# Eight weight loads, four parts of each kind and four gate tiles for the filling work that follows attention, in a one-core hybrid RWKV-7 / latent-attention block

## The chip, the core and the metric

The kernel runs on one core of one Trainium2 chip. The metric is device time in microseconds (us): the median of several runs of the same program. One further execution was taken with the hardware profiler; its rows are what the prediction argues from. The engines are called as the profile calls them: PE (matrix multiply; its loading of the stationary operand is the row PEld), DVE (vector), ACT (scalar), POOL, and SP, which issues nearly all transfers here. A wait at the head of SP's queue holds everything behind it.

## What is computed

One layer of a hybrid block on 256 latent and 256 context tokens, D = 2048. Each normed and modulated stream goes through one wide projection; one branch is a bidirectional RWKV-7 scan, the other a multi-head latent attention; both are projected to D and merged by sigmoid gates, and an output projection and a gated residual follow. What matters here is the merge at the end:

```python
def merge_branches(o_rwkv, o_mla, gate_logits, w_br_r, w_br_m, w_out):
    g_r, g_m = jnp.split(jax.nn.sigmoid(gate_logits), 2, axis=-1)
    return (g_r * (o_rwkv @ w_br_r) + g_m * (o_mla @ w_br_m)) @ w_out
...
        (rkv_x, zr_x, wd_x, ad_x, qd_x, kvd_x, kr_x, zm_x, mg_x) = project_stream(x, norm_w[i], sh_x, sc_x, w_in[i])
...
        x_new = x + g_x * merge_branches(o_rw_x, o_ml_x, mg_x, w_branch_rwkv[i], w_branch_mla[i], w_out[i])
```

`gate_logits` is `mg_x`, the last 2 x 2048 columns of the wide projection. The RWKV output `o_rw_x` is known before attention begins, the attention output only when attention is done.

## The kernel before

**Split operands.** Every large product is made of three fp32r matmuls. A weight piece `w` (128 x 512 fp32, 256 KB) is loaded by SP (`piece`, L217), then `parts_of` makes two parts of it: ACT casts the high part `wh`, DVE subtracts to give the low part `wl` (both recorded at the helper's line L122). `mm3` then issues activation-high x weight-high, activation-high x weight-low and activation-low x weight-high (L103). A piece of four 128-column blocks thus gives 12 matmuls of 128 x 256 in the work described here, and PE needs both parts of a piece before it can finish the first three of them.

**Buffers.** The list `place` says where `w`, `wh` and `wl` live and how many of each there are. It begins as `[wp, NW, NSP, NSL]`: pool `wp`, 4 loads, 3 high parts, 2 low parts. The numbers `NWL, NSX, NSX` = 8, 4, 4 are used in the pool `mg`, which is opened when attention's pool `ml` has been given back.

**Stages.** After the RWKV part (with its background projections) comes attention, in pool `ml`, until 1090 us. Beside it runs a generator `background()`, `bg`, that is advanced by `next(bg)` between steps of attention and issues *filling work*:

- `merge_gate_g(i)`: one 128-column block of the gate logits. Four pieces of `w_proj`, 48 matmuls into an `acc` tile, then ACT's tanh into a tile `th`, stored to DRAM as `thd[i]` (L454). It yields after every sixth matmul, and so takes eight steps and an end.
- `branch_g(j)`: block j of the RWKV output's projection. It loads the gate `thd[j]` back into a `th` tile (L1376), loads two pieces of `w_br[0, j]`, does 24 matmuls into `acc`, multiplies on DVE (`th = (th + 1) * acc`) and stores `th` to `thd[j]` again (L1385). There are 16 of these.

When attention is done, `for _ in bg: pass` issues all of the filling work that is left: four `merge_gate_g` blocks not yet begun on PE, and all 16 `branch_g` blocks. All of it draws on `place` as it stands, with four loads, three high and two low parts; `th` has two buffers in `wp`. So the third `th` load must wait until the first tile has been multiplied and its store has landed.

**The merge loop** `for j in range(KT)` then does block j of the attention output's projection: two pieces of `w_br[1, j]`, two gate loads `gth0`, `gth1` (L1425), 24 matmuls into `chp`, four DVE steps and a cast that write `mh`, `mlo`. At `j == 2` it sets `place[:] = mg, NWL, NSX, NSX`. After it the output projection runs over 64 pieces of `w_out`, 6 matmuls of 128 x 512 each.

**What sets the order.** The program is written in one order, and a scheduler places each engine's instructions; loads may be placed well ahead of their use where their buffer is free. `gx` and `xr` (256 KB each, L1441 and L1452) are loads for the very end.

Of the kernel before, what the change touches and what calls it, by code (L numbers as in the profile page):

```python
# [9 lines left out]
F32 = mybir.dt.float32  # L10
# [6 lines left out]
P = 128  # L17
D = 2048
KT = D // P
T = 256  # L20
# [32 lines left out]
NW, NSP, NSL, NWL, NSX, NWU, UN, NWM = 4, 3, 2, 8, 4, 4, 2, 11  # L53
# [73 lines left out]
def hybrid_block(  # L127
# [27 lines left out]
    wp = ctx.enter_context(tc.tile_pool(name="wp", bufs=2))  # L155
# [42 lines left out]
    def split(src, hi, lo):  # L198

        S.copy(hi, src)  # L200
        V.tensor_tensor(lo, src, hi.bitcast(F32), ALU.subtract)
# [10 lines left out]
    place = [wp, NW, NSP, NSL]  # L212
# [15 lines left out]
    def weights(src, n, pool=None, ns=None):  # L228

        ws = [piece(src[:, n // 2 * i:n // 2 * i + n // 2], [P, n // 2], pool) for i in range(2)]  # L230
        for w in ws:
            yield parts_of(w, pool, ns)

    def mm3(ps, ah, al, bh, bl, start, stop):

        E.matmul(ps, lhsT=ah, rhs=bh, start=start, stop=False)
        E.matmul(ps, lhsT=ah, rhs=bl, start=False, stop=False)
        E.matmul(ps, lhsT=al, rhs=bh, start=False, stop=stop)
# [334 lines left out]
    with tc.tile_pool(name="rw", bufs=1) as rw:  # L573
# [507 lines left out]
        def background():  # L1081

            while main or extra:
                ready = next((m for m in main if m[0]()), None)
                if ready:
                    main.remove(ready)
                    task = ready[1]
                elif extra:
                    task = extra.pop(0)
                else:  # L1090
                    yield False
                    continue
                for r in task:
                    yield True
                yield True

        bg = background()
# [36 lines left out]
    with tc.tile_pool(name="ml", bufs=2) as ml:  # L1134
# [227 lines left out]
        def bring():  # L1362
# [7 lines left out]
            nonlocal brought  # L1370
            brought = True

        def branch_g(j):

            th = wp.tile([P, T], F32, name="th", tag="th", bufs=2)
            nc.sync.dma_start(th, thd[j])  # L1376
            ps = pp.tile([P, 512], F32, name="acc", tag="acc", bufs=2)
            for i, (wh, wl) in enumerate(weights(w_br[0, j], 1024)):
                for k in range(4):
                    cs = slice(128 * k, 128 * k + 128)  # L1380
                    mm3(ps[:, 0:T], wh[:, cs], wl[:, cs], *(t[:, 4 * i + k] for t in ob[0]), i + k == 0, i * 4 + k == 7)
                    if k % 2:
                        yield
            V.scalar_tensor_tensor(th, th, 1.0, ps[:, 0:T], ALU.add, ALU.mult)
            nc.sync.dma_start(thd[j], th)  # L1385

        brought = False
        for j in range(KT):
            main.append(((lambda j=j: brought and len(extra) == 0), branch_g(j)))
# [14 lines left out]
    mg = ctx.enter_context(tc.tile_pool(name="mg", bufs=2))  # L1404
    ob.append(halfs(mg, [P, 8, T], "ob", 1))
    for q in range(2):
        qs = slice(4 * q, 4 * q + 4)
        split(omla[:, qs], *(t[:, qs] for t in ob[1]))
    for _ in bg:
        pass  # L1410
    while gate_left:
# [6 lines left out]
    mh = mg.tile([P, KT, T], F32R, name="mh", bufs=1)  # L1418
    ml_ = mg.tile([P, KT, T], F32R, name="mlo", bufs=1)
    for j in range(KT):  # L1420
        if j == 2:
            place[:] = mg, NWL, NSX, NSX
        th = [mg.tile([P, T], F32, name=f"gth{b}") for b in range(2)]
        for b in range(2):
            nc.sync.dma_start(th[b], thd[16 * b + j])  # L1425
        ps = pp.tile([P, 512], F32, name="chp", tag="ch", bufs=2)
        for i, (wh, wl) in enumerate(weights(w_br[1, j], 1024)):
            for k in range(4):
                cs = slice(128 * k, 128 * k + 128)
                mm3(ps[:, 0:T], wh[:, cs], wl[:, cs], *(t[:, 4 * i + k] for t in ob[1]), i + k == 0, i * 4 + k == 7)  # L1430
        t = mg.tile([P, T], F32, name="gt")
        V.scalar_tensor_tensor(t, th[1], 1.0, ps[:, 0:T], ALU.add, ALU.mult)
        V.tensor_tensor(t, t, th[0], ALU.add)
        V.tensor_scalar(t, t, 0.5, None, ALU.mult)
        split(t, mh[:, j], ml_[:, j])
# [140 lines left out]
```

## Time and profile before

| | us |
|---|---|
| median of 3 runs | 1314.25 |
| lowest, highest | 1313.71, 1323.96 |
| the profiled execution's own time | 1313.59 |
| its span, first to last instruction | 1311.5 |
| granted TensorE clock, mean of the span | 0.993 |

The stages at the end, from the span's start: attention's last DVE instruction starts at 1089.84 us; the gates that are left, to about 1120.6; the 16 branch blocks, to 1173.48; the merge loop, to 1219.66; the output projection, to 1306.91. In a row such as `1120.00:1140.00 20.00, 19.08 (x150) ...` the busy time of each engine follows the length of the stretch, then the granted clock, the share of time the core's 16 DMA engines were busy, and GB/s. Matmuls overlap: one is shown as 280 ns long although the next starts 117 ns later, so a PE that is 95% busy in such rows has lost more than 5% of its time, and the lost time is read from the pace of starts.

### The profile page before, as it was taken

How to read it: one execution, taken by the hardware profiler on the slowest of the kernel's cores; microseconds unless marked ns; L12 is line 12 of the kernel's file. 1: busy time of each engine (PE TensorE's matmuls, PEld its weight loads, DVE VectorE, ACT ScalarE, POOL GpSimd, SP SyncE). 2: the span in 40 equal slices, each digit the busy share in tenths (PEclk: the TensorE clock that was granted, in tenths of full speed). 3: DMA queues.
4: the chain of work that ended last, by engine and by line, in shares of the span. 5: the costliest groups of instructions: out<-in, count | busy, mean ns of one | idle time of the engine just before them, and what ended most of it. 6: DMA issues, size and time to landing. Idle time of an engine off the chain costs nothing.

```text
span 1311.5 us, 30092 instructions
## 1 busy us (share of the span) xinstructions
PE 1243.7 (95%) x11484; PEld 1042.2 (79%) x11484; DVE 948.6 (72%) x2658; ACT 570.6 (44%) x1183; POOL 3.3 (0%) x9
## 2 busy tenths in 40 slices
PE   6999989999999899999999998999899999989998
PEld 2656878778888778877788787888788888889887
DVE  3444875878797788887978886875877776458655
ACT  3344542443444334524434345344565555335443
POOL 0000000000000000000000000000000000000000
PEclk9999999989999999999999999999999999999999
DMA  9998345443444433424434344334843227878784
GB/s 374 339 351 316 125 141 144 144 112 111 123 124 120 123 95 109 140 76 124 123 109 129 92 130 129 99 85 121 266 137 101 85 82 223 260 233 253 216 263 143
DMA packets 172319, 212.09 MB, mean 162 GB/s; under 512 B 68560, under 2 KB 96848, under 8 KB 171664
## 3 DMA queue, kind: packets, MB, share of 16 engines
q1 hardware_dynamic: 172176, 210.18, 52.3%
q8 instruction: 90, 1.47, 0.5%
q14 instruction: 53, 0.43, 0.1%
HBM read 195.30 MB, written 14.82 MB: 160 GB/s over the span
## 4 chain that ended last, share of the span: by engine, by line
PE 63%; DMA 16%; DVE 15%; ACT 3%; issue 2%; SPq 1%; DVEq 0%; ACTq 0%
PE acc L103 27%; PE chp L103 11%; PE lv L103 9%; PE wk L103 6%; DMA wm<-in_w_mod_ss 4%; DVE wl L122 4%; PE a L103 3%; PE ch L103 3%; DMA w<-in_w_proj 2%; DVE BK L122 2%; DMA th<-thd 2%; PE wk L107 2%; DMA thd<-th 2%; DVE wt L122 1%; DMA gd<-gT 1%
## 5 line engine op out<-in xcount | busy, mean ns | idle before, releaser
L122 ACT CAST wh<-w 128x512 fp32r<-128x512 f32 (+1 forms) x484 | 291.0, 607 | 364.8 <-PE acc L103 130.7
L103 PE MATMUL acc<-hmh,wh 128*128 128x256 f32 (+1 forms) x1328 | 423.3, 319 | 11.0 <-ACT wh L122 6.6
L122 DVE TENSOR_TENSOR wl<-w,wh 128x512 fp32r<-128x512 f32 (+1 forms) x480 | 321.7, 674 | 144.2 <-ACT wh L122 77.9
L103 PE MATMUL acc<-hmh,wl 128*128 128x256 f32 (+1 forms) x1312 | 402.9, 307 | 6.4 <-DVE wl L122 5.9
L103 PE MATMUL acc<-hml,wh 128*128 128x256 f32 (+2 forms) x1328 | 405.5, 306 | 0.0
L103 PEld LDWEIGHTS acc<-hmh,wh 128*128 128x128 f32 x1328 | 251.7, 190 | 38.1 <-issue 12.5
L103 PEld LDWEIGHTS acc<-hmh,wl 128*128 128x128 f32 x1312 | 248.6, 190 | 25.7 <-DVE wl L122 12.0
L103 PEld LDWEIGHTS acc<-hml,wh 128*128 128x128 f32 (+1 forms) x1328 | 251.3, 189 | 11.4 <-issue 0.7
L122 DVE TENSOR_TENSOR pr<-wt 64x14 f32<-64x14 f32 (+6 forms) x224 | 42.7, 190 | 2.8
L122 DVE TENSOR_TENSOR wt<-wt,pr 64x14 f32<-64x14 f32 (+6 forms) x224 | 42.4, 189 | 2.3
L103 PE MATMUL pm<-wm,ssil 128*32 128x256 f32 x512 | 35.4, 394 | 6.0 <-DMA wm<-in_w_mod_ss 5.8
L103 PE MATMUL a<-hmh,wh 128*128 128x512 f32 x96 | 40.7, 424 | 0.0
L122 DVE TENSOR_TENSOR W<-WT,lv 128x512 f32<-128x512 f32 x48 | 32.8, 684 | 9.6 <-PE lv L103 9.1
L103 PE MATMUL a<-hmh,wl 128*128 128x512 f32 x96 | 38.0, 396 | 0.2 <-DVE wl L122 0.2
L103 PE MATMUL a<-hml,wh 128*128 128x512 f32 x96 | 37.9, 395 | 0.0
L103 PE MATMUL chp<-obh,wl 128*128 128x256 f32 x128 | 36.3, 284 | 0.0
L103 PE MATMUL chp<-obl,wh 128*128 128x256 f32 x128 | 36.2, 283 | 0.0
L103 PE MATMUL chp<-obh,wh 128*128 128x256 f32 x128 | 36.2, 283 | 0.0
L103 PEld LDWEIGHTS lv<-W,Z 64*64 64x64 f32 x1024 | 31.3, 135 | 3.6 <-issue 1.2
L122 ACT ACTIVATE hx<-hx,mod 128x256 f32<-128x256 f32 x32 | 17.5, 594 | 37.8 <-DVE mod L122 37.8
L122 DVE TENSOR_TENSOR AQ<-wk,cc 128x256 f32<-128x256 f32 (+1 forms) x48 | 24.4, 509 | 13.1 <-PE wk L103 12.8
L103 PE MATMUL lv<-W,Z 64*64 64x64 f32 x1024 | 33.8, 220 | 0.0
(314 smaller groups left out, 2108.2 us busy)
## 6 DMA issues: line engine op xcount, KB each, us to landing
w<-in_w_proj SPq DMA_DIRECT2D x296, 256.0 KB, 2.9
wm<-in_w_mod_ss SPq DMA_DIRECT2D x64, 512.0 KB, 8.1
w<-in_w_mod_g SPq DMA_DIRECT2D x64, 256.0 KB, 3.4
w<-in_w_br SPq DMA_DIRECT2D x64, 256.0 KB, 3.9
w<-in_w_out SPq DMA_DIRECT2D x64, 256.0 KB, 3.2
w<-in_w_first SPq DMA_DIRECT2D x32, 192.0 KB, 4.9
thd<-th SPq DMA_DIRECT2D x48, 128.0 KB, 3.2
xT<-in_xcT SPq DMA_DIRECT2D x4, 1024.0 KB, 5.5
```

The lines of the kernel that those rows point to most:

```text
L103: return self.engine.matmul(out, lhsT=lhsT, rhs=rhs, **kw)
L107: return self.engine.transpose(*a)
L122: return fn(out, *a, **kw)
```

## The change

The point at which the buffers change is moved forward, from the third round of the merge loop to a point twelve `next(bg)` steps after attention's end; and from there `branch_g` takes its `th` tiles from `mg`, four of them, since it now calls `logits()`, a name that is bound anew before the rest of the work is issued.

```diff
@@ -1370,9 +1370,12 @@
+        def logits():
+            return wp.tile([P, T], F32, name="th", tag="th", bufs=2)
+
         def branch_g(j):
 
-            th = wp.tile([P, T], F32, name="th", tag="th", bufs=2)
+            th = logits()
             nc.sync.dma_start(th, thd[j])
...
@@ -1406,6 +1409,14 @@
     for q in range(2):
         qs = slice(4 * q, 4 * q + 4)
         split(omla[:, qs], *(t[:, qs] for t in ob[1]))
+
+    for _ in range(12):
+        next(bg, None)
+    place[:] = mg, NWL, NSX, NSX
+
+    def logits():
+        return mg.tile([P, T], F32, name="th", tag="th", bufs=4)
+
     for _ in bg:
         pass
     while gate_left:
@@ -1418,8 +1429,6 @@
     for j in range(KT):
-        if j == 2:
-            place[:] = mg, NWL, NSX, NSX
         th = [mg.tile([P, T], F32, name=f"gth{b}") for b in range(2)]
```

PE's instructions stand in the same order in both programs; what moves is SP's queue, and with it ACT's and DVE's. No instruction is added or dropped on these engines. In the rows below the numbers tell buffers apart: `w_14326`, `w_14328` are the last two pieces of the first of the four gate blocks that are left, `w_14366` to `w_14556` the twelve of the other three, `w_14596` to `w_15213` those of the branch blocks, and `w_15258` onward those of the merge loop. `[waits ...]` names the semaphores that an instruction waits for (DMAHW0 to 7: earlier transfers). Lines 1376 and 1385 of the kernel before are 1379 and 1388 of the changed one.

The first place is SP's queue at attention's end, before:

```order
L217 DMA w_14328<-in_w_proj 128x512 [waits DMAHW6_49,DMAHW1_49,DVE_49]
L1425 DMA gth1_15254<-thd_1348 128x256 [waits DMAHW7_49,DVE_49]
L1425 DMA gth1_15301<-thd_1348 128x256
L217 DMA w_15352<-in_w_br 128x512
L217 DMA w_14366<-in_w_proj 128x512 [waits DMAHW2_49,DVE_49]
L217 DMA w_15354<-in_w_br 128x512 [waits DMAHW3_49]
L454 DMA thd_1348<-th_14286 128x256 [waits DMAHW4_49,Activation_49]
L217 DMA w_14368<-in_w_proj 128x512 [waits DMAHW5_49,DVE_49]
L217 DMA w_15399<-in_w_br 128x512 [waits DMAHW6_49]
L217 DMA w_14402<-in_w_proj 128x512 [waits DMAHW7_49,DVE_49]
L217 DMA w_15401<-in_w_br 128x512 [waits DMAHW0_49]
L217 DMA w_14404<-in_w_proj 128x512 [waits DMAHW1_49,DVE_49]
```

and now:

```order
L217 DMA w_14328<-in_w_proj 128x512 [waits DMAHW6_49,DMAHW1_49,DVE_49]
L217 DMA w_14366<-in_w_proj 128x512 [waits DMAHW7_49,DVE_49]
L217 DMA w_14368<-in_w_proj 128x512
L217 DMA w_14402<-in_w_proj 128x512
L217 DMA w_14404<-in_w_proj 128x512 [waits DMAHW2_49]
L217 DMA w_14442<-in_w_proj 128x512 [waits DMAHW3_49]
L217 DMA w_14444<-in_w_proj 128x512 [waits DMAHW4_49]
L217 DMA w_14478<-in_w_proj 128x512 [waits DMAHW5_49]
L217 DMA w_14480<-in_w_proj 128x512 [waits DMAHW6_49]
L454 DMA thd_1348<-th_14286 128x256 [waits DMAHW7_49,Activation_49]
L217 DMA w_14518<-in_w_proj 128x512 [waits DMAHW0_49,DVE_49]
L217 DMA w_14520<-in_w_proj 128x512 [waits DMAHW1_49,DVE_49]
```

Pieces of the merge loop (`w_15352` and on, twelve in all) stood between the pieces that PE needs next, each of which waited for DVE to give a buffer back; now the eight free buffers of `mg` take the next eight gate pieces in a row, and the merge loop's pieces follow the branch blocks'.

The second place is ACT at the same moment, before:

```order
L122 CAST wh_14330<-w_14326 128x512 [waits DMAHW5_49,PE_49,Activation_49]
L122 ACTIVATE th_14286<-acc_14189 128x256 [waits DMAHW6_49,PE_49]
L122 CAST wh_15356<-w_15352 128x512 [waits DMAHW1_49]
L122 CAST wh_14346<-w_14328 128x512 [waits DMAHW6_49,DVE_49,PE_49]
L122 CAST wh_15372<-w_15354 128x512 [waits DMAHW3_49]
L122 CAST wh_14370<-w_14366 128x512 [waits DMAHW2_49,DVE_49,PE_49]
L122 CAST wh_14386<-w_14368 128x512 [waits DMAHW5_49,DVE_49,PE_49]
L122 CAST wh_15403<-w_15399 128x512 [waits DMAHW6_49]
```

and now:

```order
L122 CAST wh_14330<-w_14326 128x512 [waits DMAHW5_49,PE_49,Activation_49]
L122 CAST wh_14370<-w_14366 128x512 [waits DMAHW7_49]
L122 CAST wh_14386<-w_14368 128x512 [waits DMAHW0_49]
L122 CAST wh_14346<-w_14328 128x512 [waits DMAHW6_49,DVE_49,PE_49]
L122 CAST wh_14406<-w_14402 128x512 [waits DMAHW1_49]
L122 CAST wh_14422<-w_14404 128x512 [waits DMAHW2_49]
L122 ACTIVATE th_14286<-acc_14189 128x256
L122 ACTIVATE th_14362<-acc_14289 128x256 [waits DMAHW4_49,PE_49]
```

In both, the cast of `w_14328` (`wh_14346`) stands behind casts of pieces in `mg`; there is now one more of these ahead of it, and the tanh `th_14286` has moved from ahead of these casts to behind four of them.

The third place is SP in the midst of the branch blocks, one round and a half, before:

```order
L1385 DMA thd_1348<-th_14921 128x256 [waits DMAHW6_49,DVE_49]
L1376 DMA th_14962<-thd_1348 128x256 [waits DMAHW0_49]
L217 DMA w_15088<-in_w_br 128x512 [waits DMAHW5_49,DVE_49]
L1452 DMA xr_16207<-in_xn 128x512
L1376 DMA th_15003<-thd_1348 128x256 [waits DMAHW7_49,DMAHW3_49]
L217 DMA w_15090<-in_w_br 128x512 [waits DVE_49]
L1385 DMA thd_1348<-th_14962 128x256 [waits DMAHW4_49,DMAHW1_49,DVE_49]
L217 DMA w_15129<-in_w_br 128x512 [waits DMAHW2_49,Activation_49]
L217 DMA w_15131<-in_w_br 128x512 [waits DVE_49]
L1385 DMA thd_1348<-th_15003 128x256 [waits DMAHW7_49,DVE_49]
```

and now:

```order
L1388 DMA thd_1348<-th_14757 128x256 [waits DVE_49]
L1379 DMA th_14880<-thd_1348 128x256 [waits DMAHW4_49,DMAHW1_49]
L217 DMA w_15008<-in_w_br 128x512 [waits DMAHW2_49,DVE_49]
L217 DMA w_15047<-in_w_br 128x512 [waits DMAHW3_49,DVE_49]
L1388 DMA thd_1348<-th_14798 128x256 [waits DVE_49]
L1379 DMA th_14921<-thd_1348 128x256 [waits DMAHW5_49,DMAHW0_49]
L217 DMA w_15049<-in_w_br 128x512 [waits DMAHW6_49,DVE_49]
L217 DMA w_15088<-in_w_br 128x512 [waits DMAHW7_49,DVE_49]
```

A load of `th` waited, before, for the landing of a store that stood only a few transfers ahead of it; now the store it waits for is that of one block earlier (for `th_14880` the store of `th_14716`, four rows ahead of the first row shown), and the tile that it fills is used three blocks later.

## The prediction

> **What bounds the kernel now.** The page's chain of work that ended last comes first:
>
> ```profile
> span 1311.5 us, 30092 instructions
> PE 63%; DMA 16%; DVE 15%; ACT 3%; issue 2%; SPq 1%; DVEq 0%; ACTq 0%
> ```
>
> PE carries it, with transfers in 16%. The change touches the time after 1090 us only, so I read the chain there, in order of time:
>
> ```profile
> 1123.84 4.29 DMA th<-thd
> 1128.12 0.02 issue
> 1128.15 0.43 DVE th L122
> 1128.58 0.02 issue
> 1128.60 2.42 DMA thd<-th
> 1131.02 0.02 issue
> 1131.04 0.02 SPq L1376
> 1131.05 0.03 issue
> 1131.08 3.34 DMA th<-thd
> ...
> 1141.58 5.06 DMA thd<-th
> ...
> 1170.43 3.04 PE acc L103 x24
> 1173.48 46.18 PE chp L103 x384
> ```
>
> Through the branch blocks the chain is no longer PE's work: load of a gate, product on DVE, store, next load. From 1173.48 on it is PE alone. What the engines did in these stages (length; PE, PEld, DVE, ACT and POOL busy; clock, DMA share, GB/s):
>
> ```profile
> 1092.80:1120.55 27.75, 25.49 (x205) 24.21 (x203) 15.02 (x23) 13.55 (x26) 0.00 (x0) 1.00 0.88 280
> 1120.55:1173.48 52.93, 47.83 (x373) 44.75 (x372) 26.56 (x47) 19.74 (x34) 0.00 (x0) 1.00 0.83 260
> 1173.48:1219.66 46.18, 46.18 (x385) 46.13 (x385) 39.69 (x92) 22.66 (x45) 0.00 (x0) 1.00 0.74 233
> ```
>
> Four gate blocks and 16 branch blocks (578 matmuls recorded) take 80.68 us; the merge loop's 385 take 46.18, or 0.120 us each, and PE never stops. The pace when nothing is late is read from a run of the same matmuls on PE's timeline, of whose 21 rows these are the first and last:
>
> ```profile
> 1089.75 0.28 PE L103 MATMUL acc<-hml,wh 128*128 128x256 f32 x1
> ...
> 1092.08 0.28 PE L103 MATMUL acc<-hmh,wh 128*128 128x256 f32 x1
> ```
>
> 2.33 us over 20 steps is 0.1165 us. I take 0.117. So 205 matmuls need 24.0 us and 373 need 43.6: 67.6 us, and 80.68 - 67.6 = 13.1 us is all that this stretch can give. Busy time shows only 2.3 + 5.1 us of it as idle, because every matmul is drawn 0.28 us long. That is 1.0% of the run, hardly more than a measurement of this kernel tells from no change, which I put at 1%.
>
> Who waits there, from 1090 to 1175 us (total, times, longest):
>
> ```profile
> ACT wh L122 <- DMA w<-in_w_br: 32.6, 25, 2.6
> DVE th L122 <- DMA th<-thd: 15.2, 13, 2.3
> SPq L217 <- DVE wl L122: 8.7, 17, 1.6
> SPq L1376 <- DMA thd<-th: 7.8, 10, 1.9
> ```
>
> ACT waits for weights that SP could not request earlier, since it waited for DVE to return one of four buffers, or stood behind a gate load that waited for a store. DVE, in order, waits for gates and holds up the low parts behind them.
>
> **The change, part by part.**
>
> *Eight loads, four and four parts.* From these issue groups (count, KB, us to landing) a load takes about 4 us:
>
> ```profile
> w<-in_w_br SPq DMA_DIRECT2D x48, 256.0 KB, 3.9
> w<-in_w_proj SPq DMA_DIRECT2D x12, 256.0 KB, 4.1
> thd<-th SPq DMA_DIRECT2D x20, 128.0 KB, 3.2
> th<-thd SPq DMA_DIRECT2D x16, 128.0 KB, 3.5
> ```
>
> A piece feeds 12 matmuls, 1.4 us. A buffer comes back about 1.3 us after the piece four before its own is through PE (0.62 us of cast, 0.69 us of subtraction). With eight buffers and four parts the new piece is requested some eight pieces, 11.3 us, before its own cast can start; less 1.3 and 4.1, 6 us are to spare. The weight waits go. In the gate blocks, where no gate is loaded, this is the whole loss: 27.75 - 24.0 = 3.8 us.
>
> *Four gate tiles.* A round of two tiles was load 3.5, product 0.43, store 3.2, at least 7.1 us for two blocks, 3.6 a block where PE needs 2.8. With four tiles it is 1.8. In the new order of SP a load waits for the store of the block before (issued 2.8 us earlier, landing after 3.2), and its tile is wanted at the end of the third block after: about 4 us to spare. Weight pieces queue behind this wait, by some 0.5 us, out of their 6. Waiting stores cannot pile up: two blocks, 5.6 us, must hold one landing plus SP's issuing, 3.2 + 1.3. So the branch blocks' loss goes as well: 52.93 - 43.6 = 9.3 us. What ends last then is PE, as in the merge loop.
>
> *The early pieces of the merge loop.* Twelve pieces, 3 MB, were loaded between 1091 and 1113 us amid pieces needed at once; now they follow in turn. Does the merge loop starve? In its second half before it lived on the same eight buffers, with two pieces and two gates, 768 KB, in each 2.89 us:
>
> ```profile
> 1206.00:1215.50 9.50, 9.50 (x81) 9.50 (x81) 8.62 (x21) 4.84 (x10) 0.00 (x0) 1.00 0.86 280
> ```
>
> PE is busy throughout, so I charge the loss of the head start with nothing; its cover is the DMA rate (second rival). The four loads of `gx` and `xr`, 1 MB, move into the gate blocks, 3.7 us of transfer at 280 GB/s, against a lead of 6 us: nothing.
>
> *Attention's end.* SP's and ACT's first rows there:
>
> ```profile
> 1090.28 1.05 SPq L1425 DMA_DIRECT2D gth<-thd  x2
> 1091.38 0.42 SPq L217 DMA_DIRECT2D w<-in_w_br  x1
> 1094.73 1.14 ACT L122 CAST wh<-w 128x512 fp32r<-128x512 f32 x2 [1.07 <-DMA w<-in_w_br]
> ```
>
> The cast of `w_14328`, needed by PE at 1096.6, was the second of the two at 1094.73, behind a piece issued at 1091.38. Now it stands behind two pieces, the first issued at 1090.28, the second 0.5 us later; with the same 3.35 us and one more load ahead of the second, they land near 1093.7 and 1094.6, and the low part is ready near 1096.6, when PE wants it within 0.3 us. The tanh `th_14286` slips to about 1097.1, and the `acc` tile it frees is wanted near 1098.1. Bounds: no stall, or, if the eight loads crowd each other, each lands 1.7 us later and PE waits as long. I take 0.5, nearer the row. PE's first matmul on an `mg` tile has a new wait for all eight transfer semaphores; before, the first matmul of the merge loop had the same, and PE did not stop there: nothing.
>
> *Crowding later.* A branch block moves two pieces, a gate in and a product out, 768 KB. 16 of them are 12.6 MB, and 384 matmuls at 0.117 are 44.9 us: 280 GB/s, just the rate of the row above. Bounds: 0, or 5.7 us if the DMAs give only the 260 GB/s of the branch row: 12.6 MB then take 48.4 us in place of 44.9, and in the merge loop 48.4 in place of 46.2 (3.5 + 2.2 us). Since 280 stood beside a PE that never stopped, I take 1.0.
>
> Sum: 13.1 - 0.5 - 1.0 = 11.6 us. The profiled execution took 1313.59 us and would take 1302.0; the median of the runs stands 0.66 above it, so 1302.6.
>
> **Rivals.**
>
> *The DMAs set the pace.* For it: shares of 0.83 to 0.88. Against it: in the same stretch SP and the tiles were what waited, and 280 GB/s was reached. At 260 the gain is 13.1 - 0.5 - 5.7 = 6.9: 1307.4.
>
> *The DMAs give less than they gave before.* Now every stage draws on them at once, without a head start. At 233 GB/s, the mean of the merge-loop row, 12.6 MB take 54.1 us, 9.2 too many in the branch blocks and 7.9 in the merge loop: the gain of 12.6 us turns into a loss of 4.5, 1318.7. Against it: that row is low because twelve pieces were there already, and its last 9.5 us had 280. The Trainium skill (DMA: Bandwidth & Descriptors, section "Bandwidth") speaks for it: it asks for 1 MiB in one DMA, at 341 GB/s, and gives 138 for 64 KB. An estimate halfway, 240 GB/s for 256 KB, would leave a loss of 1 us. The trace does not bear it out: 280 was reached with loads of 256 and 128 KB, several in flight.
>
> *The gate cycle still holds.* If stores land after 5.06 us, the longest in the chain above, one landing plus SP's 1.3 us fill 6.4 us of two blocks, 3.2 a block: 16 x 0.4 = 6.4 us of the gain go, 1309.0. The median of 3.2 speaks against it.
>
> *It does not do what it says.* If `mg`'s memory came free late, or each new wait took the place of an old one, the loss stays: 1314. Against it: the first loads into `mg` already went out at 1090.28.
>
> *Slower: PE's clock.* A denser PE might be granted less. The granted clock (third number from the end) fell twice in the middle of the run:
>
> ```profile
> 180.00:200.00 20.00, 15.34 (x111) 13.07 (x112) 16.47 (x53) 9.48 (x21) 0.00 (x0) 0.85 0.49 149
> 260.00:280.00 20.00, 17.84 (x132) 16.70 (x131) 10.19 (x26) 7.37 (x15) 0.00 (x0) 0.83 0.49 141
> ```
>
> One such 20 us stretch at 0.83 costs 4 us. The gain is gone at 0.85 over 65 us of the dense tail (11.6 / (1/0.85 - 1)), and 1% is lost at 140 us: 1327. Against it: both falls came where PE was idle, and 133 us of solid work from 1173 on ran at 1.00. The Trainium skill (TensorE: Matmul & The Clock Gate, section "The HAM clock gate") says that idleness throttles and "activity releases the throttle"; these rows agree.
>
> **How the numbers follow.** My forecast, PE back to its pace with small stalls, 0.74: 1302.6, by itself 1300.8 to 1305. The DMAs set the pace 0.11, they give less than before 0.02, the gate cycle 0.05, nothing gained 0.05, the clock 0.03. The low end is the whole 13.1 us and 0.3 of scatter, 1300.8. Upward, 1308.5 takes in the DMA rival's price and leaves out rates a little under it (0.04), the low rates, the cycle, the change without effect and the clock: 0.19 in all. Faster by over 1% means below 1301.1, a stretch with no stall at all: 0.10. Slower by over 1% needs the clock or starving far worse than any row: 0.03. Within 1%: 0.87.
>
> **What would show it.** Gate blocks done near 1116 us; a merge loop that starts near 1162 and lasts 46 us as before; DVE's 15.2 us wait for gates gone, ACT's wait for `w_br` turned into waits for PE. A chain that names `th` and `thd` would show the cycle; PE waiting for low parts behind transfers, at shares over 0.9, the DMAs; a clock under 1.00 after 1090 us, the last. A merge loop longer than 47 us would prove the head start was worth something.

## The result: 1302.2 us, a ratio of 0.9894

| | before | changed |
|---|---|---|
| median, us | 1314.89 (the 3 runs above and one of 1315.54) | 1302.18 (4 runs, 1297.50 to 1304.10) |
| ratio, 95% interval | | 0.9894 (0.9865 to 0.9922) |
| profiled execution, us | 1313.59 | 1297.50 |
| span, us | 1311.5 | 1295.7 |
| filling stretch, us | 83.7 | 70.2 |
| merge loop, us | 46.18 | 46.08 |

A second series, of six runs of the changed kernel, gave 1298.28 against 1311.99, a ratio of 0.9893 (0.9859 to 0.9926). By the ratio the change gains 1.06%; the two medians alone give 1302.18 / 1314.89 = 0.9903, a gain of 0.97%. Both intervals contain the 1% that the prediction took for its bound. Ratios and their intervals leave out a run far above the others of its kernel; there was one, in a later experiment.

The *stretch* in this table, and in all that follows, runs from the first filling matmul after attention's last product to the first matmul of the merge loop: 1089.80 to 1173.48 us before. It begins 3.0 us earlier than the 80.68 us of the prediction, in which the first matmuls of that filling were still undisturbed.

The page of the changed kernel, its chain of work that ended last by engine:

```profile
span 1295.7 us, 30060 instructions
PE 66%; DVE 15%; DMA 13%; ACT 3%; issue 2%; SPq 1%; DVEq 0%; ACTq 0%
```

Transfers fell from 16% of the chain to 13%. Its end, in order of time (start, length, what):

```profile
1086.34 1.30 PE chp L103 x11
1087.64 70.20 PE acc L103 x600
1157.85 46.08 PE chp L103 x384
```

The loads, products and stores of gates that filled the chain before have left it; the 600 matmuls of the stretch stand in one piece, 70.20 / 600 = 0.117 us each, the pace that the prediction read from 21 rows. What the engines did there (columns as in the prediction):

```profile
1092.80:1120.55 27.75, 27.75 (x238) 27.66 (x238) 15.54 (x24) 14.36 (x26) 0.00 (x0) 1.00 0.95 320
...
1120.00:1140.00 20.00, 20.00 (x174) 20.00 (x173) 12.65 (x21) 9.11 (x15) 0.00 (x0) 1.00 0.91 281
1140.00:1160.00 20.00, 20.00 (x173) 20.00 (x173) 12.79 (x22) 8.89 (x15) 0.00 (x0) 1.00 0.92 282
...
1157.85:1203.93 46.08, 46.08 (x385) 46.08 (x385) 40.55 (x93) 24.42 (x48) 0.00 (x0) 1.00 0.87 271
```

In these rows PE is busy in every microsecond, at a clock of 1.00. The same 27.75 us window holds 238 matmuls now and held 205 before, and the DMAs moved 320 GB/s in it where they had moved 280. In the branch blocks they move 281, and the merge loop, without its head start, 271 in place of 233. Who waits, from 1090 to 1160 us (total, times, longest):

```profile
ACT wh L122 <- PE acc L103: 26.5, 35, 0.9
...
ACT wh L122 <- DMA w<-in_w_br: 5.4, 7, 0.8
...
DVE th L122 <- PE acc L103: 2.7, 16, 0.2
```

ACT's casts wait for PE to give a part back, and hardly for weights (32.6 us before). DVE's gates wait for PE's sum, and the 15.2 us in which DVE waited for a gate's transfer are gone. SP itself still waits for stores, 9.9 us in all and 0.8 us a time where the prediction had 0.5; the pieces behind it have that to spare. Two groups of issues of this stretch (count, KB, us to landing):

```profile
w<-in_w_br SPq DMA_DIRECT2D x44, 256.0 KB, 4.3
thd<-th SPq DMA_DIRECT2D x21, 128.0 KB, 4.2
```

Both land later than before (stores 4.2 us after issue in place of 3.2, weights 4.3 in place of 3.9), and PE does not notice: the leads are longer than the delays.

Of the 15.8 us between the two spans, 13.5 lie in the stretch and 0.1 in the merge loop. Another 2.16 us were there already when the stretch began (1087.64 against 1089.80), in a part of the program that the change leaves alone; the profiles of this study reach that point anywhere from 1085.84 to 1097.33 us.

### The profile page after: what moved, and what is told of

It is laid out like the page before. It is cut to its first block, busy times and chain, and to the rows that moved or that the text cites. A ratio compares the mean times of both kernels' runs of the same rounds, so it can differ in the third digit from the quotient of the medians.

```text
span 1295.7 us, 30060 instructions
## 1 busy us (share of the span) xinstructions
PE 1238.3 (96%) x11484; PEld 1040.8 (80%) x11484; DVE 949.4 (73%) x2658; ACT 571.1 (44%) x1183; POOL 3.3 (0%) x9
## 4 chain that ended last, share of the span: by engine, by line
PE 66%; DVE 15%; DMA 13%; ACT 3%; issue 2%; SPq 1%; DVEq 0%; ACTq 0%
PE acc L103 31%; PE chp L103 11%; PE lv L103 9%; PE wk L103 6%; DMA w<-in_w_proj 5%; DMA wm<-in_w_mod_ss 4%; PE a L103 4%; DVE wl L122 4%; PE ch L103 3%; DVE BK L122 2%; PE wk L107 2%; ACT wh L122 1%; DVE wt L122 1%; PE pm L103 1%; DMA xT<-in_xcT 1%
## 5 line engine op out<-in xcount | busy, mean ns | idle before, releaser
L122 DVE TENSOR_TENSOR AQ<-wk,cc 128x256 f32<-128x256 f32 (+1 forms) x48 | 24.4, 509 | 13.1 <-PE wk L103 12.7
```

Of the source, the lines that this page charges most:

```text
L122: return fn(out, *a, **kw)
```

## The experiments

All kernels below are the changed one with the edit shown. Where it says "one execution", the kernel ran once, and its total carries the scatter just named; there the stretch, read from the chain of that profile, is what is compared.

### Eight loads, with two gate tiles as before

```diff
-        return mg.tile([P, T], F32, name="th", tag="th", bufs=4)
+        return wp.tile([P, T], F32, name="th", tag="th", bufs=2)
```

> The stretch is the time from the first filling matmul after attention's last product to the first matmul of the merge loop: 83.7 us before (1089.80 to 1173.48), 70.2 us with the change (1087.64 to 1157.85). Theory (two causes, gate cycle the larger): with eight loads and four parts but only two gate tiles, the four gate blocks stay at PE's pace (about 28 us from 1087.6, as now), and the branch blocks are held by load, product, store of two tiles, 7.1 to 8.3 us for two blocks, so 53 to 60 us: stretch 79 to 88 us, 9 to 18 us longer than with the change, and the chain names th and thd. Rival (the weight loads were the cause, the gate tiles only came along): stretch at most 73 us.

Measured: 1308.98 us (10 runs) against 1314.96, ratio 0.9953 (0.9923 to 0.9983); stretch 80.0 us. Its chain, in order of time:

```profile
1089.86 19.78 PE acc L103 x167
...
1116.05 2.91 DMA th<-thd
...
1119.49 2.69 DMA thd<-th
...
1122.20 3.17 DMA th<-thd
...
1161.88 4.31 DMA th<-thd
...
1166.83 3.04 PE acc L103 x24
```

The gate blocks run at PE's pace, so their loss was one of weights. From 1116 us on the chain is again load, product, store, load. From the load at 1116.05 to that at 1161.88 the chain goes round seven times, 6.55 us a round of two blocks, 3.3 a block where PE needs 2.8. The theory holds, with a round a little shorter than the 7.1 us it gave: with two tiles the gate cycle alone costs 9.8 us.

### Four gate tiles, with the loads and parts as before

```diff
-    place[:] = mg, NWL, NSX, NSX
...
     for j in range(KT):
+        if j == 2:
+            place[:] = mg, NWL, NSX, NSX
```

> Four gate tiles in the merge's memory, loads and parts as before (4, 3, 2). Theory: the gate blocks lose their 3.8 us as before; in the branch blocks a piece is requested about 4.3 us before its cast can start and lands after 3.9 to 4.5, so they come near PE's pace with small stalls, 45 to 49 us in place of 52.9: stretch 76 to 80 us. Rival (weights were the cause): branch blocks as before, stretch 82 to 85 us. Rival (gate tiles were everything): stretch near 73 to 74 us.

Measured: 1313.23 us (10 runs), ratio 0.9988 (0.9961 to 1.0016); stretch 83.4 us. Its chain in the branch blocks:

```profile
1122.57 6.77 DMA w<-in_w_br
...
1135.24 4.88 DMA w<-in_w_br
...
1142.39 5.27 DMA w<-in_w_br
```

The theory missed here: it gave the gates a share of their own, and the share is nothing. The rival had the size. The chain no longer names gate loads but weights, at nearly the pace that the gates had set. So two limits lay one behind the other: taking away the weights' alone shortens the stretch by 3.7 us, the gates' alone by 0.3, both by 13.5. The other 9.5 us belong to neither part; they are had with both or not at all. "The weights' alone" is here the whole of the moved line: eight loads, four parts of each kind, and the merge loop's pieces behind the urgent ones.

### Four loads, in four and four parts

```diff
-    place[:] = mg, NWL, NSX, NSX
+    place[:] = mg, NW, NSX, NSX
```

This holds in the merge loop and the output projection as well, where the kernel before had eight.

> The change with four loads instead of eight in the merge's memory, four parts of each kind kept; this holds for the merge loop and the output projection as well. Theory: with four parts a piece is split as soon as the piece four before it is through PE, so the request comes about 4 pieces (5.6 us) before the cast can start, less 1.3: 4.3 us against a landing of 4.3 to 4.5 at the present DMA rate. Stretch 71 to 76 us, merge loop 46 to 51 us, with ACT waiting for w_br. Rival (eight loads are what counts): stretch 80 us or more, merge loop over 52 us. Rival (four parts alone suffice): stretch 70 to 71, merge loop 46.

Measured, one execution: 1305.66 us. Windows of the stretch and of the output projection:

```profile
1087.70:1162.40 74.70, 73.11 (x621) 72.41 (x619) 41.75 (x69) 33.53 (x57) 0.00 (x0) 1.00 0.83 257
...
1209.70:1303.00 93.30, 88.62 (x385) 71.36 (x383) 52.54 (x84) 38.22 (x62) 0.00 (x0) 1.00 0.66 211
```

The stretch proper takes 72.6 us, from 1089.84 (the first row begins 2.1 us ahead of it, at the last products), the merge loop 47.3, both within the theory's ranges, and the output projection 93 in place of 87. So the last four loads are worth 2.4 us in the stretch, 1.2 in the merge loop and 6 in the output projection. The experiment before this one had four loads as well, and took 10.8 us more in the stretch; it had fewer parts, and the merge loop's early pieces stood among the urgent ones. Where the 10.8 us lie can be read from DVE's gate products (the experiment before, then this one):

```profile
L122 DVE SCALAR_TENSOR_TENSOR th<-th,acc x16: 411/414/416, 1121.6 to 1175.0; 128x256 f32<-128x256 f32 x16
L122 DVE SCALAR_TENSOR_TENSOR th<-th,acc x16: 411/414/416, 1119.1 to 1164.2; 128x256 f32<-128x256 f32 x16
```

From the first product to the merge loop's first matmul it was 51.4 us there and is 43.3 here, so 8.1 of the 10.8 us lie in the branch blocks. SP had issued the early pieces by 1122 us, so there the parts remain, beside the four loads for the very end (`gx`, `xr`), which lie among the branch blocks there and ahead of them here. In the gate blocks, the other 2.7 us, no run takes parts and order apart.

### Eight loads, in three high and two low parts

```diff
-    place[:] = mg, NWL, NSX, NSX
+    place[:] = mg, NWL, NSP, NSL
```

> The change with eight loads but three high and two low parts, in the merge loop and the output projection too. Theory: with two low parts the subtraction of piece n can start when piece n-2 is through PE and ends 1.3 us later (cast 0.62, subtraction 0.69), 0.1 us before piece n is begun and 0.35 before its low part is needed; where DVE is also busy with a gate product (0.42 us) it comes late by up to 0.4 us once a block. Stretch 70 to 77 us, merge loop 46 to 53 us since DVE has more to do there. Rival (parts are as needed as loads): stretch 80 us or more.

Measured, one execution: 1296.82 us; stretch 70.77, in one piece of PE's work:

```profile
1085.84 70.77 PE acc L103 x600
1156.60 46.07 PE chp L103 x384
```

Beside eight loads the additional parts are worth 0.6 us at most. The stretch of these kernels, cut at DVE's first gate product (us):

| | to the first product | from there to the merge loop |
|---|---|---|
| before | 33.2 | 50.5 |
| two gate tiles | 29.1 | 50.9 |
| four gate tiles alone | 32.0 | 51.4 |
| four loads | 29.3 | 43.3 |
| few parts | 29.1 | 41.7 |
| the change | 28.3 | 41.9 |

In the branch blocks neither half of the change gains anything by itself.

### Three gate tiles

```diff
-        return mg.tile([P, T], F32, name="th", tag="th", bufs=4)
+        return mg.tile([P, T], F32, name="th", tag="th", bufs=3)
```

> Three gate tiles instead of four. With the change the store takes 4.2 us to land, the gate load 3.7, the product 0.42: 8.3 us a round. Theory (the round is shared by the tiles): 8.3 / 3 = 2.8 us a block, PE's own 2.81, so the cycle just about holds: stretch 70 to 73 us. Rival (what counts is one tile more or less in the queue, as SP stands behind each store): 74 us or more.

Measured, one execution: 1300.39 us; stretch 70.8. Its chain:

```profile
1092.72 5.46 DMA w<-in_w_proj
...
1098.61 62.06 PE acc L103 x528
1160.67 9.35 PE chp L103 x78
```

No gate is in the chain: a third tile is enough. The 0.6 us stand at the start, where a piece took 5.46 us to land and the tanh behind its cast gave PE its `acc` tile back late. That is the stall at attention's end that the prediction charged with 0.5 us, by the second of the two ways it named; it shows here and, as 1.0 us and by the first way (a late low part), in the kernel with the operand spread out, below, and in neither profile of the changed kernel.

### One more load in each branch block

An extra piece of 256 KB is loaded with each gate, into a tile that nothing reads; what is computed is the same.

```diff
+        def extra_load(j):
+            pass
...
             th = logits()
             nc.sync.dma_start(th, thd[j])
+            extra_load(j)
...
+    def extra_load(j):
+        t = mg.tile([P, 512], F32, name="xl", tag="xl", bufs=4)
+        nc.sync.dma_start(t, w_br[0, j][:, 0:512])
```

> The change with one more 256 KB load for each branch block, of which nothing is computed (a piece of w_br into a tile that nobody reads): 4.2 MB more in the stretch, 24.9 MB where 20.7 were moved. At 70.2 us that asks for 355 GB/s, and 373 in the branch blocks. Theory (the DMAs have little room: 331 GB/s at 0.97 was the most over 20 us): at 331 GB/s the 24.9 MB take 75 us, the stretch is 73 to 78 us, and ACT waits for w_br. Rival (the DMAs were far from their limit): stretch 70 to 71 us.

Measured, one execution: 1308.73 us; stretch 75.5, 5.3 longer. Two windows of it, and ACT's wait for weights from 1090 to 1170 us:

```profile
1120.00:1140.00 20.00, 20.00 (x173) 20.00 (x173) 13.04 (x22) 8.71 (x14) 0.00 (x0) 1.00 0.91 290
1140.00:1160.00 20.00, 16.47 (x136) 15.85 (x135) 8.11 (x16) 6.21 (x10) 0.00 (x0) 1.00 0.87 269
...
ACT wh L122 <- DMA w<-in_w_br: 17.4, 12, 3.1
```

The length is as the theory had it, and ACT waits for `w_br` (17.4 us, 5.4 in the changed kernel by 1160 us), but the DMAs are not at their most: when PE begins to stop, the DMAs move 269 to 290 GB/s, less than they moved in the gate blocks of the changed kernel. (Nor were the theory's 331 GB/s the most of the run: the first four slices of the changed kernel's page, 32 us each, have 308 to 375.) Its chain there:

```profile
1139.83 4.11 DMA thd<-th
1143.95 0.33 SPq L1382
...
1145.49 4.15 DMA thd<-th
```

L1382 is the load of a gate, waiting on SP for a store that takes 4.1 us to land, with the weights in the queue behind it: the additional load brings the wait for stores back before the DMAs are at their most. It is a third more traffic (256 KB on 768) and one more transfer for SP to issue; together they use up the changed kernel's spare time, and this run does not say which does it.

### Without the twelve steps ahead of the move

```diff
-    for _ in range(12):
+    for _ in range(0):
```

> The change without the twelve steps: the buffers are the merge's at once. Theory: the pieces that PE needs next (from w_14250 on) can only be asked for when attention has given its memory back, 0.5 us after its last product; they land 3.5 us later and are split 1.3 us after that, so PE stands for 4 to 6 us at the start and the stretch is 74 to 77 us. Rival (the place of the switch does not matter): 70 to 71 us.

Measured, one execution: 1306.49 us; stretch 77.6. Its chain, and two windows of PE at that place:

```profile
1087.88 1.32 PE chp L103 x11
...
1089.67 3.98 DMA w<-in_w_proj
...
1093.67 0.63 ACT wh L122
...
1094.34 72.50 PE acc L103 x600
```

```profile
1094.34:1100.00 5.66, 5.66 (x29) 5.44 (x30) 3.37 (x5) 2.91 (x5) 0.00 (x0) 0.60 0.83 287
1100.00:1105.00 5.00, 5.00 (x45) 5.00 (x45) 2.67 (x4) 2.33 (x5) 0.00 (x0) 1.00 0.60 189
```

PE stands from 1089.20 to 1094.34, 5.1 us, until a piece has come into memory that is free only when attention is done. The wait is what the theory gave; the stretch is 0.6 us longer than its range, for a reason that it did not have: after the stop the granted clock is 0.60 in the mean of 5.66 us, with 29 matmuls where the next 5.00 us hold 45; 5.66 x 0.40 = 2.3 us more. Both together are the 7.4 us that the twelve steps are worth, over half of what the change gains.

### The merge loop's operand in attention's memory

This and the next test the one thing that PE's chain still shows, 0.120 us for a matmul of the merge loop against 0.117 in the stretch. The moving operand is put where the stretch has its own:

```diff
-    ob.append(halfs(mg, [P, 8, T], "ob", 1))
+    ob.append([t[:, 0:8, T:TT] for t in (hmh, hml)])
```

> The change, with the merge loop's moving operand (both parts of the attention output) placed in the tiles of the stream's parts, whose columns attention has just left, instead of in the merge's memory. The merge loop's matmuls start 0.120 us apart, the branch blocks', which have the same shape and read those tiles, 0.117, although PE waits for nothing in either. Theory (where the moving operand lies): merge loop 44.9 to 45.2 us in place of 46.1. Rival (DVE's greater load there, or the transfers): 46.1 us still.

Measured, one execution: 1294.49 us. The chain and the window of the merge loop:

```profile
1087.45 68.60 PE acc L103 x588
1156.05 14.00 PE chp L103 x120
```

```profile
1156.05:1200.85 44.80, 44.80 (x386) 44.80 (x385) 40.39 (x93) 24.73 (x48) 0.00 (x0) 1.00 0.92 294
```

44.80 / 384 = 0.1167 us. DVE and ACT are as busy as in the changed kernel's 46.08 us, and the DMAs faster: neither explains the slower pace, the place of the operand does. The stretch is 1.6 us shorter, 1.4 of it because the chain counts 588 matmuls in it in place of 600.

The same kernel, timed in several runs:

> The change with the merge loop's moving operand in the stream's tiles, timed in rounds. Theory: 1.3 us less than the change alone by the merge loop (46.1 to 44.8), ratio 0.9887 to before, not told from the change alone by the clock on the wall but by the merge loop's length. Rival (the one look's low time was its own): at least 3 us less than the change.

Measured: 1296.68 us (median of 6 runs, one of which took 3953.5 us; 1294.24 without it) against 1311.99, ratio 0.9860 (0.9828 to 0.9892; five runs), and the merge loop 44.80 us again. By the five runs it lies 4.0 us below the changed kernel, which is the rival's size and not the theory's 1.3. But its interval overlaps the changed kernel's of the same series (0.9859 to 0.9926), so the times neither tell the two kernels apart nor decide between theory and rival; the merge loop does show the theory's share, 44.80 us in two profiles against 46.07 and 46.08.

### The same operand, spread out

```diff
-    ob.append(halfs(mg, [P, 8, T], "ob", 1))
+    ob.append([t[:, :, 0:T] for t in halfs(mg, [P, 8, T + 64], "ob", 1)])
```

> The change with the merge loop's moving operand still in the merge's memory, but its eight blocks laid 320 columns apart instead of 256, so that they do not touch. Theory (blocks that touch or an even spacing make the slower pace): merge loop 44.8 to 45.1 us. Rival (it is the region of memory): 46.1 us as with the change.

Measured, one execution: 1299.70 us. From its chain:

```profile
1089.81 5.22 DMA w<-in_w_proj
...
1160.01 46.08 PE chp L103 x384
```

The first row is the late landing at attention's end, the second the merge loop. Blocks that lie apart are as slow as blocks that touch, so this theory falls. What is left is the region of memory, or the spacing of 512 columns that the operand has in the other place, which no run tried here; why one place is slower than another stays open.

### The change once more

> The changed kernel once more, beside the next, for the size of the difference in time: in the one profile the stretch gave 13.5 us and the parts of the program before it another 2.2 us that the change does not touch. Theory (only the stretch): 13.5 us less than before, ratio 0.9897, and the same stretch of 70 to 71 us in the profile. Rival (the change also speeds what comes before): 15 us or more, ratio 0.988 or lower.

Measured: 1298.28 us (6 runs) against 1311.99, ratio 0.9893 (0.9859 to 0.9926): 13.7 us less, near the theory's 13.5 and short of the rival's 15. The execution that was profiled took 1307.16 us, and shows where such differences lie:

```profile
1097.33 70.16 PE acc L103 x600
...
0.00:900.00 900.00, 848.24 (x8742) 686.07 (x8743) 664.70 (x1985) 364.25 (x773) 3.31 (x9) 0.98 0.49 150
```

The stretch is the same to 0.04 us, though it begins 9.7 us later than in the first profile. The clock up to 900 us is 0.98 here and was 0.99 there. By the means of the whole span, 0.988 and 0.993, an estimate of what the clock took is 0.005 of 1305 us, 6.5 us; the rest of the 9.7 is not explained.

## Why the prediction was right

The forecast (PE back to its pace) is what happened, and 1302.6 stands against a median of 1302.18. Point by point:

- *What bounds the kernel, and 13.1 us to be had*: right. The stretch fell by 13.5 us, to the pace that was read from the 21 rows.
- *Eight loads, four and four parts, the gate blocks' 3.8 us*: right in size, and shown apart from the tiles: with two gate tiles the gate blocks run at PE's pace and the stretch gains 3.7 us. The number of loads is not what does it: with four loads and four parts the time to the first gate product is 29.3 us, with eight and few parts 29.1, with both 28.3, and 33.2 before. What these kernels share beside is that the merge loop's pieces no longer stand among the urgent ones; whether that alone would have been enough no run shows.
- *Four gate tiles, the branch blocks' 9.3 us*: right as a sum, but it was put down to the tiles. Alone they gain 0.3 us in the stretch and nothing in the branch blocks, since weights with four buffers and few parts are as slow as the gates were. The sentence "the weight waits go", in the part on the loads, was a condition of it. The expectation of that experiment repeated the slip, and missed.
- *Head start of the merge loop, nothing*: right, 46.08 us against 46.18.
- *Attention's end, 0.5 us*: nothing in the two profiles of the change, 0.6 and 1.0 us in two near relatives. The bounds (none, or 1.7) hold. What covers it are the twelve steps, which the prediction did not price: without them PE stands 5.1 us and the clock falls.
- *Crowding, 1.0 us*: mis-sized, it is nothing. The prediction took the 280 GB/s of one row for the rate to count on; the DMAs gave 320 over 27.75 us with PE at its pace. The trace of the kernel before already had more: 333 GB/s from 1095 to 1100 us, and 316 to 374 in the first four slices of its page. The estimate from the Trainium skill (DMA: Bandwidth & Descriptors, section "Bandwidth"), 240 GB/s for loads of 256 KB, is lower still. Its table is measured with transfers issued from GpSimd, and here SP issues them, several in flight; which of the two makes the difference no run shows.
- *Rivals*: none came true. The gate cycle needed stores of 5.06 us, and they land after 4.2; with one more load a block it does come back. The clock stayed at 1.00.
- *The time and the chances*: the profiled execution is 4.5 us below the 1302.0 worked out for it: 1.5 are the two terms that came to nothing, 2.2 PE's earlier arrival, 0.4 the stretch's size, 0.4 the rest of the run. "Within 1%" had 0.87; by the ratios both series lie at 1.06 to 1.07%, just beyond, where the prediction itself had put a stretch with no stall at all, and by the medians of the first series 0.97%, just inside. Which side of 1% it falls on is within the scatter of these runs. A gain worked out at 1.0% with two small losses taken off should have had its chances divided more evenly about that bound.

## What to carry to other kernels

Where two buffers run short at nearly the same pace, the chain names only one, and relieving that one gains little: work out each cycle's time per block beside the pace wanted, and relieve all that exceed it before judging any. When loads are to move into memory that comes free only at the end of a stage, keep enough work in the old place to cover the first landing. To price a denser stage, take the DMA rate from the densest stretch of the trace that was not short of requests, for a rate measured where buffers were short is no ceiling (280 GB/s here, then 320).

## What was not expected of the hardware

**A stop of 4.7 us costs the clock, stops of up to 2.5 us do not.** PE's longest wait at attention's end in the kernel without the twelve steps (total, times, longest):

```profile
PE acc L103 <- ACT wh L122: 4.7, 1, 4.7
```

The 0.60 over the next 5.66 us is a mean of two levels. Single microseconds of the same trace (the first during the stop):

```profile
1093.00:1094.00 1.00, 0.00 (x0) 0.00 (x0) 0.16 (x1) 0.33 (x1) 0.00 (x0) 0.50 0.66 219
...
1098.00:1099.00 1.00, 1.00 (x6) 1.00 (x6) 0.41 (x1) 0.55 (x1) 0.00 (x0) 0.55 1.05 404
1099.00:1100.00 1.00, 1.00 (x11) 1.00 (x10) 0.28 (x1) 0.44 (x1) 0.00 (x0) 1.00 0.40 152
```

The clock fell to 0.50 while PE stood, and was 1.00 again from about 1099 us on, some 5 us after PE had work. In the kernel with two gate tiles PE stopped often, and for a shorter time:

```profile
PE acc L103 <- DVE th L122: 7.9, 6, 2.5
```

```profile
1120.00:1140.00 20.00, 16.71 (x139) 16.24 (x138) 9.18 (x18) 7.01 (x12) 0.00 (x0) 1.00 0.78 240
```

Its clock stayed at 1.00. This agrees with the Trainium skill (TensorE: Matmul & The Clock Gate, section "The HAM clock gate"), which has the throttle come back after an idle window of about 3.4 us.

**The pace depends on where the moving operand lies.** The same 384 matmuls take 46.08 us with it in the merge's memory and 44.80 in attention's. The weight loads differ too. Two rows of PE's loads by tile (minimum, median and maximum ns), of the changed kernel:

```profile
L103 PEld LDWEIGHTS chp<-obh,wh x128: 187/192/192, 1157.6 to 1203.3; 128*128 128x128 f32 x128
```

and of the one with the operand moved:

```profile
L103 PEld LDWEIGHTS chp<-hmh,wh x128: 187/188/189, 1155.8 to 1200.2; 128*128 128x128 f32 x128
```

192 ns against 188, though the weights are in the merge's memory in both.
